# Latent attention with TensorE kept in program order, its last attention set apart, and modulation weights loaded two dot products ahead

## The chip, the cores and the metric

The kernel runs on one core of a Trainium2 chip. Its time is the device time of one execution in microseconds (us); three executions of the kernel before were timed, and one more was profiled. The core's engines are PE (TensorE, matrix products), DVE (VectorE), ACT (ScalarE), POOL (GpSimd) and SP (SyncE, which here only issues DMAs).

## The reference

One layer of a diffusion backbone for 256 latent tokens, with 256 context tokens ahead of them, of width 2048. What matters here:

```python
def reference(...):
    sh1, sc1, g1, sh2, sc2, g2 = jnp.split(jax.nn.silu(c) @ w_ada[l] + b_ada[l], 6, axis=-1)
    (lq_a, lkv_a, lk_r, ldq, ldk, ldv, ldz, lda, ldb, lga, lgb) = split_columns(
        modulate(rmsnorm(x, norm_mix[l]), sh1, sc1) @ w_in[l])
    ...
    k_l, v_l = mla_kv(lkv_a, lk_r, kv_a_norm[l], w_kv_b[l], k_norm[l], tabs)
    q_l = mla_q(lq_a, q_a_norm[l], w_q_b[l], q_norm[l], tabs)
    y_mla_l = attend_latent(q_l, k_l, v_l, k_c, v_c)
    ...
    o_dn_l, _ = dn_bidirectional(lq, lk, lv, lgd, lbeta, s_ctx, True)
    y_l = merge_branches(y_mla_l, dn_output(o_dn_l, ldz, ...), lga, lgb, w_o_mla[l], w_o_dn[l], w_out[l])
    x = x + jnp.expand_dims(g1, -2) * y_l
    x = x + jnp.expand_dims(g2, -2) * conv_glu(modulate(rmsnorm(x, norm_ffn[l]), sh2, sc2), ...)
```

`mla_kv` and `mla_q` normalise a latent of rank 512, multiply it up to 8 heads of 128 + 64 columns, normalise each head and rotate the last 64 columns (the rope). `attend_latent` is a softmax attention over 512 keys.

## The kernel before

**Stages.** By the trace the first projection and the first part of the modulation run to about 150 us, the heads of the gated DeltaNet to 440, the latent attention (MLA) from 440 to 743, the DeltaNet's scan to 957, the two branch projections and the output projection to 1145, and the feed-forward part to the end.

**Weights.** Every weight matrix comes as tiles of 128x1024 (`raw`, five places, shared with the `rawa` tiles below). `split` (L118) makes of each half of such a tile a rounded high part `whi` by a copy on ACT (L120) and the rest `wlo` by a subtraction on DVE (L121); there are six places for such halves. PE multiplies with both. All PE work goes through one helper, so that all its rows bear line 68.

**The latent attention.** Heads are taken in four pairs, b = 0 to 3. `mla_project(b)` (L984) makes keys (`k_head`, products `kps`), their norms (`ks`, `kbp`), values (`vps`), queries (`q_tile`, products `qps`) and the rotated parts of the queries (`rps`, which reads `qx`). `mla_attend(b)` (L1087) makes four tiles of scores (`sps`; two heads by two blocks of 128 queries). For each, DVE takes the maximum (L1102, L1104), ACT the exponential (L1105), DVE the reciprocal (L1106) and ACT the scaled row `s_` (L1107). `turn` transposes it on PE (`ptp`) and splits it into `PT` (ACT L120, DVE L121); `values` multiplies it with the values (`yps`) and sends the result to DRAM (`Ys`), from where it comes back as `yraw` and is split into `YM`.

**Side work.** Both generators give a number of ns at each `yield`, and `side(c, r)` (L1147) then issues as much of three other things: `fill`, the products `gtp` of z and gate tiles with the projected stream `h`, 24 tiles of 16 pairs of products; `inv`, products `ivp` of the blocks of an inverse that the scan needs (`off_diagonal`, L831, results to DRAM as `Xo`); and `ada`, the late modulation (`ada_rest`, L253). That is 128 dot products on DVE (L278) of a weight tile `rawa` with a row `sch`; each reads a tile that SP loads one dot ahead (L259). The loop at L1153 to L1162 first runs `mla_project(0)` through, then takes one step of `mla_project(b+1)` and one of `mla_attend(b)` by turns, seven times for each b. In the last round nothing is left to project.

**What sets the order.** A scheduler orders the instructions of every engine by its own times, where the code does not pin them. With `pe.pinned` True, PE's instructions stay in the order of the program; before the change that holds in the heads and in the scan, but not in the latent attention. Each engine then works through its order strictly, and an instruction that waits holds up those behind it. DVE, ACT and SP are left to the scheduler here.

Of the kernel before, what the change touches and what calls it, by code (L numbers as in the profile page):

```python
# [41 lines left out]
OC = 4000  # L42
# [11 lines left out]
def hybrid_block(ctx: ExitStack, tc: tile.TileContext, io, dbg=None):  # L54
# [20 lines left out]
    pe, oact, odve = (Ordered(e) for e in (nc.tensor, nc.scalar, nc.vector))  # L75
# [4 lines left out]
    def pool_(name, bufs, side="left"):  # L80
        return tc.tile_pool(name=name, bufs=bufs, side=side, reuse_waits="tile")
# [20 lines left out]
    half = const.tile([P, 1], F32, name="half")  # L102
# [150 lines left out]
    def ada_rest():  # L253


        def load(i):
            w = wr.tile([P, GR], F32, tag="raw", name="rawa", bufs=NR)
            c, n = divmod(i, 32)
            sync.dma_start(w, io["wada2"][c, (n // 16 + c) % 2, n % 16])  # L259
            return w  # L260

        parts = ad.tile([P, 2, 16], F32, name="parts")
        half, ahead = None, load(0)
        for i in range(128):
            c, n = divmod(i, 32)
            h, j = (n // 16 + c) % 2, n % 16
            if h != half:

                for _ in range(2 if i else 0):
                    yield 1300  # L270
                half, sch = h, ad.tile([P, GR], F32, tag="sch", name="sch")
                sync.dma_start(sch, Sc[h])
                for _ in range(4):
                    yield 1300
            w = ahead
            if i < 127:
                ahead = load(i + 1)
            dve.tensor_tensor_reduce(out=w, in0=w, in1=sch, scale=1.0, scalar=0.0, op0=ALU.mult, op1=ALU.add, accum_out=parts[:, h, j : j + 1])  # L278
            if n == 31:
                cs = slice(16 * c, 16 * c + 16)  # L280
                dve.tensor_tensor(out=adaT[:, cs], in0=parts[:, 0], in1=parts[:, 1], op=ALU.add)
                dve.tensor_tensor(out=adaT[:, cs], in0=adaT[:, cs], in1=bada[:, 32 + 16 * c : 48 + 16 * c], op=ALU.add)
                ada.done = c + 1
            yield 1300
# [124 lines left out]
    def load(*what):  # L409
        for kind, n in what:  # L410
            d, f = {"w": (wts, load_scale), "s": (shifts, load_shift), "g": (grs, load_first)}[kind]
            d[n] = f(n)
# [342 lines left out]
    def head_inputs(h, side=lambda c: None):  # L755
# [13 lines left out]
        return xs[0], xs[1], xq  # L769

    ada = Side(ada_rest())
    ada.done = 0
    ins = {h: head_inputs(h) for h in (3, 0)}
# [9 lines left out]
    for heads, nxt in (((3, 0), (4, 1)), ((4, 1), (5, 2)), ((5, 2), (6,)), ((6,), (7,)), ((7,), ())):  # L783
# [3 lines left out]
        def side(c):  # L787
            work(c * 17000 * len(heads) / main)
            ada(c * ADB / 22600)
# [41 lines left out]
    def off_diagonal():  # L831

        pI = ExitStack()
        pi = pI.enter_context(pool_("pj", 1, "right"))
        bd = [pi.tile([P, 4, P], F32, name=f"bd{n}") for n in range(2)]
        for n in range(2):
            pool.memset(bd[n], 0.0)

        def load(q):
            rs = slice(4 * q, 4 * q + 4)  # L840
            uo = pi.tile([P, 4, 32], F32, tag="uo", name="uo", bufs=2)
            sync.dma_start(uo, Uo[:, :, rs].rearrange("g j r i -> (g j) r i"))
            xd = pi.tile([P, 2, 4, 32], F32, tag="xd", name="xd", bufs=2)
            for n in range(2):
                sync.dma_start(xd[:, n], Xq[2 * n, rs].rearrange("r g j c -> (g j) r c"))
            return uo, xd

        ahead = load(0)
        yield OD
        for q in range(8):  # L850
            uo, xd = ahead
            if q < 7:
                ahead = load(q + 1)
            for n in range(2):
                src = uo if n == 0 else ip
                for g in range(4):
                    gs = slice(32 * g, 32 * g + 32)
                    act.copy(bd[n][gs, :, gs], src[gs])
                ip = psa.tile([P, 4, 32], F32, tag="aux", name="ivp")
                for r in range(4):  # L860
                    pe.matmul(ip[:, r], bd[n][:, r], xd[:, n, r], start=True, stop=True)
                if n == 0:
                    yield OC
            act.copy(uo, ip)
            act.dma_start(Xo[4 * q : 4 * q + 4].rearrange("r g c i -> (g c) r i"), uo)
            yield OC
        pI.close()

    Ys = dram.tile([P, HEADS, T], F32, name="Ys")
# [90 lines left out]
    pN.close()  # L960
    pc2 = pC.enter_context(pool_("pc2", 2))
    inv = Side(off_diagonal())

    def mm3(ps, a, b, first, last):
# [19 lines left out]
    def mla_project(b):  # L984
# [41 lines left out]
        def q_tile(j):  # L1026
            ps = psa.tile([P, 512], F32, tag="aux", name="qps")
            for k in range(4):
                mm_hl(ps, P, W(j * 512 + k * P), qan_[:, k], k == 0, k == 3)
            qx = pc2.tile([P, T], F32, tag="qx", name="qx")  # L1030
            gather(ps, P, qx)
            if j < 2:
                act.activation(qts[j][:, 0], qx, AF.Copy, scale=qkn)
                dve.scalar_tensor_tensor(out=qts[j][:, 1], in0=qx, scalar=qkn, in1=qts[j][:, 0], op0=ALU.mult, op1=ALU.subtract)
            act.activation(qsq[:, j], qx, AF.Square)
            return qx
# [25 lines left out]
            pass  # L1062
        yield 3500
        qx = q_tile(2)
        yield 1300
        rps = psa.tile([P, T], F32, tag="aux", name="rps")
        pe.matmul(rps, perm, qx, start=True, stop=True)
        rq = ryx[:, 0]
# [78 lines left out]
    def side(c, r):  # L1147
        fill(r * c)
        inv(r * c)
        ada(AD * c)  # L1150

    for c in mla_project(0):
        side(c, R0)  # L1153
    for b in range(4):
        at, pr = mla_attend(b), mla_project(b + 1) if b < 3 else iter(())
        for n in range(7):
            for st in (pr, at):
                c = next(st, None)
                if c is not None:
                    side(c, R1 if b < 3 else 2.0)  # L1160
        for _ in at:
            pass  # L1162
    inv.finish()
    fill.finish()
    gates = gate_tiles([("wgd", f, Gs[1, :, f], None) for f in range(KD)])
# [407 lines left out]
```

## Time and profile before

| | us |
|---|---|
| median of three executions | 1846.19 |
| lowest and highest | 1843.73, 1850.49 |
| the profiled execution | 1845.3 |
| its span in the trace | 1843.5 |
| PE busy | 1773.1 |
| DVE busy | 1366.4 |
| ACT busy | 917.9 |

All times of rows are of the profiled execution, in us from the start of its span, which lies 1.8 us within that execution's time. Rows of a timeline give start, duration, engine, line, operation, out<-in, partitions x elements, and in brackets the idle time just before the instruction and what ended it. Matrix products overlap: what one adds is the distance to the start of the next, not its duration.

### The profile page before, as it was taken

Reading aid. Unit: us, or ns where it says so; the run is one execution under the profiler, and the core shown is the slowest. Engines: PE = TensorE matmul, PEld = TensorE weight load, DVE = VectorE, ACT = ScalarE, POOL = GpSimd, SP = SyncE. Lnnn points to the kernel's source line nnn. Section 1 sums busy time; section 2 is a strip of 40 time slices with the busy share of each in tenths; the row PEclk is TensorE's granted clock in tenths of the full one; section 3 lists DMA queues with packets and bytes.
Section 4 is the critical chain, followed back from the end, with each engine's and each line's share of the span. In section 5 each row is a group of like instructions: output and inputs, shape, how many; then the busy total and the mean of one; then the engine's idle time right before and its main releaser. Section 6 shows DMA issues by size and latency. Waiting matters only on the chain.

```text
span 1843.5 us, 33058 instructions
## 1 busy us (share of the span) xinstructions
PE 1773.1 (96%) x12450; PEld 1525.7 (83%) x12450; DVE 1366.4 (74%) x2758; ACT 917.9 (50%) x1876; POOL 45.9 (2%) x48
## 2 busy tenths in 40 slices
PE   7999999999998999898999989999999999999999
PEld 5787887888887888777878877888888888888887
DVE  4668899879776877575779798888877788855554
ACT  3335544445666665433346445555555555544443
POOL 0000001000000000000000000000000000000000
PEclk9999999999999999999989999999999999999999
DMA  9883688774777767887766885777766677766664
GB/s 379 349 311 110 178 241 241 215 235 132 214 229 222 217 209 227 293 287 244 250 220 206 285 297 179 254 220 223 231 197 187 212 219 221 266 194 195 201 197 120
DMA packets 195009, 419.72 MB, mean 228 GB/s; under 512 B 61280, under 2 KB 101344, under 8 KB 192416
## 3 DMA queue, kind: packets, MB, share of 16 engines
q1 hardware_dynamic: 167520, 402.19, 68.0%
q10 hardware_dynamic: 27328, 15.41, 2.8%
q8 instruction: 98, 1.61, 0.4%
q14 instruction: 63, 0.52, 0.1%
HBM read 388.57 MB, written 28.84 MB: 226 GB/s over the span
## 4 chain that ended last, share of the span: by engine, by line
PE 48%; issue 9%; DVE 2%; DMA 2%; ACT 1%; POOL 0%; SPq 0%; POOLq 0%; ACTq 0%; DVEq 0%
PE fps L68 25%; PE dps L68 13%; PE gtp L68 4%; PE brp L68 2%; PE op L68 1%; DVE wlo L121 1%; DMA raw<-in_wgate 1%; PE yp L68 1%; DMA yraw<-Ys 0%; DVE r L1264 0%; PE kp L68 0%; ACT whi L120 0%; DMA Gs<-zx 0%; POOL om L172 0%; DMA raw<-in_wgd 0%
## 5 line engine op out<-in xcount | busy, mean ns | idle before, releaser
L121 DVE TENSOR_TENSOR wlo<-raw,whi 128x512 fp32r<-128x512 f32 (+1 forms) x940 | 634.5, 686 | 209.7 <-ACT whi L120 202.0
L120 ACT CAST whi<-raw 128x512 fp32r<-128x512 f32 (+1 forms) x940 | 572.9, 618 | 420.8 <-PE dps L68 112.4
L68 PE MATMUL fps<-H,whi 128*128 128x512 f32 x1376 | 481.5, 398 | 1.7 <-DVE H L1416 1.7
L68 PE MATMUL fps<-H,wlo 128*128 128x256 f32 x1376 | 374.3, 282 | 0.6 <-DVE wlo L121 0.6
L68 PEld LDWEIGHTS fps<-H,whi 128*128 128x128 f32 x1376 | 253.8, 189 | 57.9 <-issue 2.0
L68 PEld LDWEIGHTS fps<-H,wlo 128*128 128x128 f32 x1376 | 259.3, 188 | 8.7 <-DVE wlo L121 1.1
L68 PE MATMUL gtp<-h,whi 128*128 128x512 f32 x640 | 234.7, 402 | 5.1 <-ACT whi L120 5.1
L68 PE MATMUL mmp<-h,whi 128*128 128x512 f32 x640 | 228.9, 400 | 0.0
L68 PE MATMUL dps<-GB,whi 128*128 128x512 f32 x560 | 195.9, 391 | 0.0
L278 DVE CUSTOM_DVE_ANT_0 rawa<-rawa,sch 128x1024 f32<-128x1024 f32 x128 | 156.2, 1222 | 44.0 <-DMA rawa<-in_wada 43.1
L68 PE MATMUL gtp<-h,wlo 128*128 128x256 f32 x640 | 175.7, 285 | 5.5 <-DVE wlo L121 5.2
L68 PE MATMUL mmp<-h,wlo 128*128 128x256 f32 x640 | 176.6, 282 | 0.0
L68 PE MATMUL dps<-GB,wlo 128*128 128x256 f32 x560 | 155.3, 282 | 0.0
L68 PEld LDWEIGHTS gtp<-h,whi 128*128 128x128 f32 x640 | 120.8, 190 | 31.5 <-ACT whi L120 6.3
L68 PEld LDWEIGHTS mmp<-h,whi 128*128 128x128 f32 x640 | 119.1, 188 | 26.2 <-issue 0.4
L68 PEld LDWEIGHTS gtp<-h,wlo 128*128 128x128 f32 x640 | 121.3, 190 | 13.2 <-DVE wlo L121 8.7
L68 PEld LDWEIGHTS dps<-GB,whi 128*128 128x128 f32 x560 | 105.2, 188 | 21.7
L68 PEld LDWEIGHTS mmp<-h,wlo 128*128 128x128 f32 x640 | 120.5, 188 | 2.8 <-issue 0.6
L68 PEld LDWEIGHTS dps<-GB,wlo 128*128 128x128 f32 x560 | 105.9, 189 | 0.6
L68 PE MATMUL fp<-h,gh 128*128 128x256 f32 (+1 forms) x448 | 86.6, 291 | 7.9 <-DVE h L68 5.9
L68 PEld LDWEIGHTS fp<-h,gh 128*128 128x128 f32 (+1 forms) x448 | 69.2, 187 | 15.1 <-DVE h L68 8.0
L513 ACT COPY fx<-fps 128x256 f32<-128x256 f32 x86 | 31.9, 374 | 68.3 <-PE fps L68 68.2
(561 smaller groups left out, 2561.9 us busy)
## 6 DMA issues: line engine op xcount, KB each, us to landing
rawa<-in_wada SPq DMA_DIRECT2D x128, 512.0 KB, 4.7
raw<-in_wgate SPq DMA_DIRECT2D x82, 512.0 KB, 4.3
raw<-in_wval SPq DMA_DIRECT2D x82, 512.0 KB, 4.8
raw<-in_wdown SPq DMA_DIRECT2D x80, 512.0 KB, 4.3
wt<-in_wadas SPq DMA_DIRECT2D x16, 1024.0 KB, 9.9
raw<-in_wadab SPq DMA_DIRECT2D x32, 512.0 KB, 8.5
raw<-in_wgm SPq DMA_DIRECT2D x32, 512.0 KB, 4.9
raw<-in_wgd SPq DMA_DIRECT2D x32, 512.0 KB, 6.1
```

Of the source, the lines that this page charges most:

```text
L68: i = f(*a, **k)
L120: act.copy(hi, raw)
L121: dve.tensor_tensor(out=lo, in0=raw, in1=hi, op=ALU.subtract)
L278: dve.tensor_tensor_reduce(out=w, in0=w, in1=sch, scale=1.0, scalar=0.0, op0=ALU.mult, op1=ALU.add, accum_out=parts[:, h, j : j + 1])
L513: act.copy(out, ps[:M, T:])
```

## The change

Loads of `rawa` are issued two dots ahead of their use in place of one. `off_diagonal` gives half of its ns before each group of products instead of all after it (the sum stays). `mla_project` gives 2600 ns in place of 1300 between the last query tile and the rotation. PE is pinned from the latent attention on, and stays so through the scan. In the loop the attention of the pair before (`tail`) is given a step between the two others; after the loop there is a `side(2600, 1.0)`, and the rest of `tail` is run. Since `mla_attend` has seven yields and is given seven steps, what is handed over as `tail` has no work left.

```diff
-        half, ahead = None, load(0)
+        half, ahead = None, [load(0), load(1)]
...
-            w = ahead
-            if i < 127:
-                ahead = load(i + 1)
+            w = ahead.pop(0)
+            if i < 126:
+                ahead.append(load(i + 2))
...
+                yield OC / 2
                 ip = psa.tile([P, 4, 32], F32, tag="aux", name="ivp")
...
                 if n == 0:
-                    yield OC
+                    yield OC / 2
...
-            yield OC
+            yield OC / 2
...
         qx = q_tile(2)
-        yield 1300
+        yield 2600
         rps = psa.tile([P, T], F32, tag="aux", name="rps")
...
+    pe.pinned = True
     for c in mla_project(0):
         side(c, R0)
+    tail = iter(())
     for b in range(4):
         at, pr = mla_attend(b), mla_project(b + 1) if b < 3 else iter(())
         for n in range(7):
-            for st in (pr, at):
+            for st in (pr, tail, at):
                 c = next(st, None)
                 if c is not None:
                     side(c, R1 if b < 3 else 2.0)
-        for _ in at:
-            pass
+        tail = at
+    side(2600, 1.0)
+    for _ in tail:
+        pass
```

**The first keys, on PE.** Before, the twelve products of the first head's keys stand woven between products `gtp`:

```order
L68 MATMUL gtp<-h_308,whi 128x512
L68 MATMUL kps<-kvn,whi 128x512
L68 MATMUL gtp<-h_308,whi 128x512
L68 MATMUL gtp<-h_308,wlo 128x256
L68 MATMUL gtp<-h_308,whi 128x512
L68 MATMUL gtp<-h_308,wlo 128x256
L68 MATMUL gtp<-h_308,whi 128x512
L68 MATMUL kps<-kvn,whi 128x512
L68 MATMUL kps<-kvn,wlo 128x512
```

After, behind the same `gtp`, they are one block:

```order
L68 MATMUL gtp<-h_308,whi 128x512
L68 MATMUL kps<-kvn,whi 128x512 x2
L68 MATMUL kps<-kvn,wlo 128x512
L68 MATMUL kps<-kvn,whi 128x512 x2
L68 MATMUL kps<-kvn,wlo 128x512
L68 MATMUL kps<-kvn,whi 128x512 x2
L68 MATMUL kps<-kvn,wlo 128x512
L68 MATMUL kps<-kvn,whi 128x512 x2
L68 MATMUL kps<-kvn,wlo 128x512
```

The `gtp` that stood between have moved behind the block.

**The last attention (b = 3), on PE.** Before, the second transposition and what is around it (the `gtp` rows that are left out here are 15 more of the same two kinds in a row, behind the first score tile shown):

```order
L68 MATMUL ptp<-ident,s__8487 128x128 x4
L68 MATMUL sps<-kt,qt 128x512 x3
L68 MATMUL sps<-krt,qt 128x512 x2
L68 MATMUL gtp<-h_308,whi 128x512
...
L68 MATMUL ptp<-ident,s__8531 128x128 x4
L68 MATMUL sps<-kt,qt 128x512 x3
L68 MATMUL sps<-krt,qt 128x512 x2
L68 MATMUL ptp<-ident,s__8579 128x128 x4
L68 MATMUL gtp<-h_308,whi 128x512
L68 MATMUL gtp<-h_308,wlo 128x256
L68 MATMUL gtp<-h_308,whi 128x512
L68 MATMUL yps<-PT,V 128x512
```

After, from the second score tile on:

```order
L68 MATMUL sps<-kt,qt 128x512 x3
L68 MATMUL sps<-krt,qt 128x512 x2
L68 MATMUL ptp<-ident,s__8550 128x128 x4
L68 MATMUL sps<-kt,qt 128x512 x3
L68 MATMUL sps<-krt,qt 128x512 x2
L68 MATMUL ptp<-ident,s__8597 128x128 x4
L68 MATMUL sps<-kt,qt 128x512 x3
L68 MATMUL sps<-krt,qt 128x512 x2
L68 MATMUL ptp<-ident,s__8618 128x128 x4
L68 MATMUL yps<-PT,V 128x512
```

No `gtp` is left between them up to the last `yps`. Of the 58 that stood there before (16 + 16 + 3 + 14 + 9), 32 have moved ahead of this attention, into the longer steps before `rps`, and 26 behind it, where 96 follow in a row in place of 70. Before `rps` there stood 8 `gtp` behind the query tile in the rounds b = 0 and 1; now there are 16 and the 4 (`ivp`) of the inverse, and more.

**The dots in that attention, on DVE.** After, a dot stands between the maximum of a score and its reciprocal (L1107, L1106 before) twice; here is the second, for the score tile 8618:

```order
L121 TENSOR_TENSOR PT<-ptp,PT 128x4x128
L1103 ISA s__8618,mns<-kbc,sps 128x512
L1103 ISA mns 128x1
L1107 RECIPROCAL mns<-mns 128x1
L1105 TENSOR_SCALAR mns<-mns,qm 128x1
L278 ISA rawa,parts<-rawa,sch 128x1024
L278 ISA parts 128x1
L1107 RECIPROCAL mns<-mns 128x1
L121 TENSOR_TENSOR PT<-ptp,PT 128x4x128
```

Before, none stands between the two (those of this attention come behind a reciprocal). A third stands after between `qm` and `qt`, ahead of the first score tile.

**Loads and dots.** On SP the second load is issued right behind the first, and each later one an index earlier at its place. On DVE the dots have moved by one index too, so that the first now stands here, among the DeltaNet heads:

```order
 L666 SCALAR_TENSOR_TENSOR cy<-ct,cy 128x256
+L278 ISA rawa,parts<-rawa,sch 128x1024
+L278 ISA parts 128x1
 L121 TENSOR_TENSOR wlo<-raw,whi 128x512 x2
```

Between the load of a tile and the dot that reads it there stand in this stage and the next about as many weight halves as before (three, before four). When the attention's result `YM` is split, 58 dots stand ahead of it, before 54.

## Rows read from the trace of the kernel before

**Rows 1.** The page's busy times of the engines over the whole span, with their share of it and their instructions.

```profile
PE 1773.1 (96%) x12450; PEld 1525.7 (83%) x12450; DVE 1366.4 (74%) x2758; ACT 917.9 (50%) x1876; POOL 45.9 (2%) x48
```

**Rows 2.** The latent attention as one stretch: its length, busy time (and count) of PE, weight loads, DVE, ACT and POOL, granted clock, DMA share, GB/s.

```profile
440.00:743.00 303.00, 288.81 (x2211) 249.57 (x2209) 222.49 (x475) 193.81 (x435) 18.98 (x18) 0.99 0.71 216
```

**Rows 3.** Waits of PE in the same stretch: who waited for what, us in total, times, the longest.

```profile
PE yps L68 <- DVE PT L121: 3.4, 2, 2.7
PE rps L68 <- DVE qx L514: 2.9, 2, 2.0
PE yp L68 <- DMA jit<-Xo: 2.2, 1, 2.2
PE ks L68 <- ACT ksq L995: 2.1, 2, 1.9
```

**Rows 4.** Waits of DVE in the same stretch, the largest.

```profile
DVE rawa L278 <- DMA rawa<-in_wada: 27.5, 22, 5.1
```

**Rows 5.** PE's timeline around the second of the two waits for `qx`, in round b = 1; the first row is the first of eight products `gtp` behind the query tile.

```profile
631.99 0.40 PE L68 MATMUL gtp<-h,whi 128*128 128x512 f32 x1
...
633.41 0.60 PE L68 MATMUL ptp<-ident,s__7451 128*128 128x128 f32 x4
635.97 0.70 PE L68 MATMUL rps<-qx,rope 128*128 128x256 f32 x2 [1.97 <-DVE qx L514]
...
637.11 0.64 PE L68 MATMUL gtp<-h,whi 128*128 128x512 f32 x1
...
641.33 0.39 PE L68 MATMUL gtp<-h,whi 128*128 128x512 f32 x1
```

**Rows 6.** DVE's timeline, ahead of PE's longest wait for `PT` (first row) and just ahead of that `rps`.

```profile
570.71 1.23 DVE L278 CUSTOM_DVE_ANT_0 rawa<-rawa,sch 128x1024 f32<-128x1024 f32 x1 [5.13 <-DMA rawa<-in_wada]
...
634.35 1.22 DVE L278 CUSTOM_DVE_ANT_0 rawa<-rawa,sch 128x1024 f32<-128x1024 f32 x1
...
635.50 0.42 DVE L514 TENSOR_TENSOR qx<-qps,qx 128x256 f32<-128x256 f32 x1
```

**Rows 7.** Three stretches at the lower granted clock, columns as in rows 2: the two of the latent attention, and one at the end of the output projection.

```profile
572.46:575.87 3.41, 3.27 (x10) 2.79 (x11) 2.45 (x8) 2.03 (x6) 1.18 (x1) 0.50 0.62 234
637.32:640.73 3.41, 3.41 (x11) 2.85 (x11) 2.12 (x7) 1.00 (x3) 1.11 (x1) 0.50 1.02 393
...
1104.94:1115.18 10.24, 5.57 (x32) 4.65 (x33) 7.20 (x18) 3.74 (x9) 0.70 (x1) 0.50 0.33 102
```

**Rows 8.** PE's timeline at the first keys: the first product of the first head, and three of the second head's.

```profile
455.55 0.50 PE L68 MATMUL kps<-kvn,whi 128*128 128x512 f32 x1
...
463.36 0.63 PE L68 MATMUL kps<-kvn,whi 128*128 128x512 f32 x2
...
464.06 0.63 PE L68 MATMUL kps<-kvn,whi 128*128 128x512 f32 x2
```

**Rows 9.** DVE's timeline there: the last of the four rows of the latent, normalised, and its low part.

```profile
458.44 0.74 DVE L955 SCALAR_TENSOR_TENSOR kvx<-kvx,vecs,bk 128x512 f32<-128x512 f32 x1
...
460.30 0.69 DVE L121 TENSOR_TENSOR kvn<-kvx,kvn 128x512 fp32r<-128x512 f32 x1
```

**Rows 10.** ACT's timeline: the high part of that row, and the squares of the first head's keys with the instruction ahead of them that waited.

```profile
459.51 0.62 ACT L120 CAST kvn<-kvx 128x512 fp32r<-128x512 f32 x1 [0.41 <-DVE kvx L955]
...
472.71 0.37 ACT L513 COPY zx<-gtp 128x256 f32<-128x256 f32 x1 [3.15 <-PE gtp L68]
...
473.90 0.58 ACT L995 ACTIVATE ksq<-kps 128x512 f32<-128x512 f32 x1
```

**Rows 11.** PE's timeline in the last attention: the first transposition, the third score tile, the product behind it, and the first product with the values.

```profile
710.34 0.60 PE L68 MATMUL ptp<-ident,s__8487 128*128 128x128 f32 x4
710.69 0.94 PE L68 MATMUL sps<-kt,qt 128*128 128x512 f32 x3
...
711.93 0.39 PE L68 MATMUL gtp<-h,whi 128*128 128x512 f32 x1
...
718.36 1.69 PE L68 MATMUL yps<-PT,V 128*128 128x512 f32 x8 [0.68 <-DVE PT L121]
```

**Rows 12.** DVE's timeline there: the maximum of that third score tile, and the low part of its `PT`.

```profile
713.55 0.68 DVE L1102 CUSTOM_DVE_ANT_0 s__8579<-kbc,sps 128x512 f32<-128x512 f32 x1
...
718.83 0.69 DVE L121 TENSOR_TENSOR PT<-ptp,PT 128x512 fp32r<-128x512 f32 x1
```

**Rows 13.** ACT's timeline there: the scaled row of the tile, and the high part of its `PT`.

```profile
715.66 0.73 ACT L1107 ACTIVATE s__8579<-s__8579,mns 128x512 f32<-128x512 f32 x1
...
718.07 0.57 ACT L120 CAST PT<-ptp 128x512 fp32r<-128x512 f32 x1
```

**Rows 14.** The chain of waits behind the last attention, in order of time: start, us, what.

```profile
726.90 4.00 DMA Ys<-ryx
730.92 7.82 DMA yraw<-Ys
738.76 1.91 ACT YM L120
740.69 2.30 DVE YM L121
```

**Rows 15.** PE's timeline at the end of the latent attention: the first products of the scan's side, and the first of the branch projection.

```profile
740.51 2.02 PE L68 MATMUL yp<-jit 128*128 128x128 f32 x16 [2.15 <-DMA jit<-Xo]
743.04 0.50 PE L68 MATMUL brp<-YM,whi 128*128 128x512 f32 x1 [0.51 <-DVE YM L121]
```

## Prediction

> **What bounds the kernel now.** I read the busy times first: PE works for 1773.1 of 1843.5 us [rows 1], so the kernel is PE's order of work and the gaps in it. A gain can only come from gaps of the stretch that is changed. The stretch of the latent attention is 303.0 us long with PE busy for 288.8 [rows 2], so at most 14.2 us are to be had there, 0.8% of the whole. The list of PE's waits says what the gaps are: `PT` 3.4 us, `qx` 2.9, the inverse coming back from DRAM 2.2, `ksq` 2.1 [rows 3]. The engine behind most of them is DVE, and DVE's own list says why: it waits 27.5 us in 22 places for a `rawa` tile that has not landed [rows 4]. Since DVE keeps to its order, a dot that waits for its tile holds up the subtraction that PE needs: the dot at 570.71 waited 5.13 us, and PE's longest wait, 2.7 us for `PT`, ended just behind it [rows 3, 6].
>
> Two more things are to be seen in the stretch. The granted clock fell to 0.50, its lower level of 1.2 GHz, for 3.41 us twice, each time behind one of the two longest waits, that of 2.73 us and that of 1.97 us [rows 3, 5, 7]; behind the 2.15 us wait for the inverse no such stretch follows. And the work that fills PE's gaps, `gtp`, is a fixed amount: what is moved into one gap is missing in another.
>
> **The change part by part.** The sum is made against the profiled execution (1845.3 us), which lies 0.9 below the median of 1846.2, so that a change of zero reads 1845.3 to 1846.2.
>
> *The longer step before `rps`.* In rounds 0 and 1 `rps` waited for `qx`, 2.9 us in two places [rows 3]. In the second, 8 `gtp` from 631.99 to 633.41 and one transposition lay between the query tile and `rps` at 635.97, and the rest was the wait [rows 5]; on DVE a dot of 1.22 us stood right ahead of `qx` [rows 6]. Eight `gtp` take 1.42 us, 0.178 each. The new order puts 16 of them there, the inverse's products and a transposition, over 3.2 us in place of 1.4 and what the latter two take, so the first wait (0.9) goes surely and the second, with 1.97, as good as: **-2.9**. The lower clock behind the second goes with it. 3.41 us at half the clock hold at most 1.7 us of lost work, and the products there were pushed to 0.64 from 0.39 us [rows 5, 7]: **-1.5** (0 to -1.7).
>
> *The pinned first keys.* Before, twelve products for the first head were woven between `gtp` from 455.55 on [rows 8]; three of them take 0.70 us, so all take 2.8. In a block they would end at 458.35. But the last row of the latent is only normalised at 458.44, has its high part at 459.51 and its low part at 460.30 to 460.99 [rows 9, 10], and DVE's and ACT's orders there have hardly moved. The low part is read by the last three products, so the block ends at about 461.5: **+3.1** in waits. The bounds are 0, if that row comes sooner once the `gtp` gathers around it are later, and +4.6, if the wait also brings a stretch of lower clock like the two above.
>
> *The squares of the first head.* `ks` waited up to 1.9 us [rows 3], since on ACT a gather of a `gtp` tile that was not done stood ahead of `ksq` (3.15 us of waiting) [rows 10]. One such gather less stands there now: **-1.1** (0 to -1.9).
>
> *The last attention.* This is the dear part. From the maximum of a score to its finished row take 713.55 to 716.39, 2.84 us [rows 12, 13]; the high and low parts of `PT` add 0.57 and 0.69. A transposition costs PE 0.35 us and a score tile 1.24 [rows 11]. Before, 16 `gtp` (2.8 us) stood behind each of the first three scores, and they and the next score hid the chain; the wait that was left was 0.68 at the first `yps` [rows 11]. Now only the first tile has them. The second row must be ready 0.35 + 1.24 = 1.6 us after its score, against 2.84 and some time for the engines to take turns: 1.3 to 1.8 us of waiting. The third has the same two pieces and the wait before it: about 0.6. The products with the values then wait for `PT`, 0.57 + 0.69 less what lies between, 1.2 and 1.3, and the first transposition may wait 0.8 for its exponential, behind a weight half that finds no free place. Together 5.7, against 0.7 in the same places before: **+5.0** (bounds +1.2, if only the wait for the second row is left, and +8, if none of the waits overlaps with another).
>
> *Behind it.* The chain by `Ys` and `yraw` to `YM` takes from 726.90 to 742.99, 16.1 us, and the gather ahead of it [rows 14]. Before, 70 `gtp` covered it and PE waited 2.15 and 0.51 us in the end [rows 15]. Now 96 do; the 26 more are 26 x 0.178 = 4.6 us, and both waits go: **-2.7**. So of the 26 products that left the attention over half comes back here.
>
> *The loads two ahead.* The text asks for a dot's tile one index sooner. But DVE's order follows what the scheduler takes as landed: dot and load both moved one index, and between them stand about as many halves as before. So the 27.5 us of waits on `rawa`, 1.25 each in 22 places, stay, and with them the long wait for `PT`, its lower clock, and the smaller waits: 0, between -4.9 (the waits for `PT` and the lower clock behind the longest gone) and +5 (another one like the longest). Three dots now stand at worse places, in the last attention: one ahead of `qt` and so of the first score, 1.23 us of its own: **+1.2**; two between a maximum and its reciprocal, where nothing hides them any more; if one of them waits the mean of 1.25, and partly beside PE's work: **+1.0** (0 to +10). Four dots fewer are left for the scan and the output projection, whose other work keeps its order: 0, with ±4 for what their places there do.
>
> *`tail`, the split `yield` of the inverse:* 0. The first has no work; the second keeps its sum, and the inverse's transfers have 16 us more of cover at the end, as above.
>
> Sum: -2.9 - 1.5 + 3.1 - 1.1 + 5.0 - 2.7 + 1.2 + 1.0 = **+2.1**. That is 1847.4 against the profiled execution and 1848.3 against the median; I say **1847**. A difference of 0.5% (9 us) is about what a measurement of this kernel can tell from no change; this is well inside.
>
> **The rivals.**
>
> *The loads do come a dot sooner (faster).* If the tiles have landed when DVE gets to the dots, the waits for `PT` (3.4) and its lower clock (1.5) go beside those for `qx`, and the dots of the last attention cost only their 1.23: 1847.4 - 3.4 - 1.5 - 1.0 = 1841.5; if the first keys hide their wait as well, 1838.4, and with the 4 us that the later dots may give, 1834. That needs DVE's waits on `rawa` to fall from 27.5 to a few us. For it: the code asks for it, and most of PE's waits have this source. Against it: the new order moved each dot with its load. And even this ends at the edge of what can be told.
>
> *The last attention stalls on dots (slower).* The two dots between maximum and reciprocal have no cover. If each waits like the longest, 5.13 us [rows 6], PE stands for 10.2 us more, in pieces of over 2 us between short groups of products. The granted clock has been at 0.50 behind such waits, and for 10.24 us at a stretch where PE was busy for only 5.57 of them [rows 7]; at half the clock such a stretch costs up to 5.1. Then 1847.4 - 1.0 + 10.2 + 5.1 = 1861.7; with one dot late and 3.41 us of lower clock, 1847.4 - 1.0 + 5.1 + 1.7 = 1853.2. It decides the sign from two dots that wait over 4 us each. Against it: of 22 waits the mean is 1.25 us. The Trainium skill ("TensorE: Matmul & The Clock Gate", section "HAM oscillation — how this bites in real kernels") speaks for it: idle gaps between short groups of matmuls send the clock to half its rate again and again, so that each group starts cold. The trace agrees in two places of the stretch and disagrees in one (2.15 us, no drop); by that rule every gap of the last attention would count, which is this rival.
>
> *The change does little of what it says.* `tail` is empty, and the loads' lead does not grow. This is not beside the forecast; it is part of it.
>
> **How the numbers follow.** The forecast, waits shifted and about even: 0.72, 1839 to 1855. The faster rival 0.14, of which some 0.10 lies below 1837, with what the scan's dots may add; the slower one 0.14, all but a little above 1855. The range of 8 in 10 takes in the unknown terms: 1847.4 less 3.1 (keys hidden), 3.8 (the attention's lower bound) and 2 (half of what the later dots may give) is some 1838, and 1847.4 plus 3 (its upper bound), 1.5 (clock at the keys) and 5 (one late dot) some 1857: 1838 to 1857. Faster by over 0.5% (below 1837) 0.10, within it 0.76, slower (above 1855.4) 0.14.
>
> **What would show it.** In the profile after: no wait of `rps` for `qx`; a block of twelve `kps` near 456 to 462 with waits for `kvn`; in the last attention waits of `ptp` for `s_` and of `yps` for `PT` of 4 to 7 us together, and none of `yp` for `jit` or `brp` for `YM` behind it; DVE's waits on `rawa` in this stretch still over 20 us. It would be wrong if those fall under 10 us (then faster), if the clock is at 0.50 for over 10 us in the last attention (then slower), or if a stage after 743 us changes by more than 4 us.

## The result and the profile after

The changed kernel takes 1855.8 us (median of six; 1850.1 to 1864.2), the kernel before 1846.9 beside it: a ratio of 1.0048, 95% interval 1.0030 to 1.0066. Measured once more on another occasion it was 1.0044 (1.0025 to 1.0063). It is slower by some 8 to 9 us, within the stated range of 1838 to 1857 and just inside the half per cent, but well above the forecast of 1847. The profiled execution, 1850.1 us with a span of 1848.3, is the shortest of the six, so its trace shows about half of the loss (its span is 4.8 us longer than before); the second profile (1858.0 us) is used beside it. One execution of that second occasion, 2474.7 us at a mean granted clock of 0.652, is left out of its ratio.

Waits of PE in the latent attention, after (columns as in rows 3):

```profile
PE ptp L68 <- ACT s__8618 L1108: 3.3, 1, 3.3
PE ptp L68 <- ACT s__8550 L1108: 2.0, 1, 2.0
PE ks L68 <- DVE mns L1103: 1.9, 1, 1.9
PE ptp L68 <- ACT s__8597 L1108: 1.7, 1, 1.7
PE yps L68 <- DVE PT L121: 1.4, 1, 1.4
PE ks L68 <- ACT ksq L996: 1.3, 3, 0.8
PE ptp L68 <- ACT s__8641 L1108: 1.1, 1, 1.1
PE kps L68 <- ACT kvn L120: 1.1, 1, 1.1
PE kps L68 <- DVE kvn L121: 1.1, 2, 0.7
```

All waits of [rows 3] for `qx`, for `jit` and the long one for `PT` are gone. In their place stand the four rows `s_` of the last attention and one `PT`, 9.5 us together, and a wait of `ks` in the third pair, 1.9 us in place of 1.2 before. PE's timeline there shows them one after another, and the products slower towards the end:

```profile
706.90 0.63 PE L68 MATMUL sps<-krt,qt 128*128 128x512 f32 x2
709.48 0.66 PE L68 MATMUL ptp<-ident,s__8550 128*128 128x128 f32 x4 [1.95 <-ACT s__8550 L1108]
...
712.97 0.66 PE L68 MATMUL ptp<-ident,s__8597 128*128 128x128 f32 x4 [1.67 <-ACT s__8597 L1108]
...
718.07 0.66 PE L68 MATMUL ptp<-ident,s__8618 128*128 128x128 f32 x4 [3.28 <-ACT s__8618 L1108]
718.48 2.09 PE L68 MATMUL yps<-PT,V 128*128 128x512 f32 x8
721.65 1.12 PE L68 MATMUL ptp<-ident,s__8641 128*128 128x128 f32 x4 [1.08 <-ACT s__8641 L1108]
724.17 2.93 PE L68 MATMUL yps<-PT,V 128*128 128x512 f32 x8 [1.40 <-DVE PT L121]
```

The last `yps` takes 2.93 us against 1.69 of the first one before [rows 11]: the granted clock is at 0.50 there, for as long as the third stretch of [rows 7] (columns as there):

```profile
719.47:729.71 10.24, 7.75 (x25) 6.04 (x24) 2.31 (x5) 2.86 (x7) 2.42 (x3) 0.50 0.22 74
```

The longest wait has a dot behind it. DVE's timeline, between the maximum of the third score and its reciprocal:

```profile
712.12 0.21 DVE L1105 TENSOR_SCALAR mns<-mns,qm 128x1 f32<-128x1 f32 x1
715.95 1.23 DVE L278 CUSTOM_DVE_ANT_0 rawa<-rawa,sch 128x1024 f32<-128x1024 f32 x1 [3.62 <-DMA rawa<-in_wada]
717.10 0.08 DVE L278 DVE_READ_ACCUMULATOR2_ANT parts<- 128x1 f32 x1
717.10 0.16 DVE L1107 RECIPROCAL mns<-mns 128x1 f32<-128x1 f32 x1
```

Over the stretch, DVE still waits over 20 us for tiles of the dots (27.5 us in [rows 4]), and for their row `sch` in one place:

```profile
DVE rawa L278 <- DMA rawa<-in_wada: 21.8, 16, 3.6
...
DVE rawa L278 <- DMA sch<-Sc: 2.2, 1, 2.2
```

Behind the attention the two waits of [rows 15] are gone:

```profile
745.08 1.95 PE L68 MATMUL yp<-jit 128*128 128x128 f32 x16
746.78 0.48 PE L68 MATMUL brp<-YM,whi 128*128 128x512 f32 x1
```

The first branch product starts at 746.8, before at 743.0. From there to the first product of the feed-forward part it is 367.6 us (1114.4), before 368.2 (1111.2), and from there to the end 733.9, before 732.3.

In what follows the attention is measured from the first `kps` to the first `brp`: 287.5 us before (455.5 to 743.0), 290.6 in the first profile after (456.2 to 746.8), 295.6 in the second (461.0 to 756.6). So of the 4.8 us that the first profile is longer, 3.1 lie in the attention, 0.7 ahead of it and 1.6 in the feed-forward part, less 0.6 between. Of the 12.7 us of the second, 8.1 lie in the attention and 5.5 ahead of it. What makes it start later is not shown: the eight profiles with the loads two ahead have their first `kps` between 455.4 and 461.0 us, the six without between 455.2 and 457.9.

### The profile page after: what moved, and what is told of

The parts are those of the page before. It is cut to its first block, busy times and chain, and to the rows that moved or that the text cites. A ratio compares the mean times of both kernels' runs of the same rounds, so it can differ in the third digit from the quotient of the medians.

```text
span 1848.3 us, 33065 instructions
## 1 busy us (share of the span) xinstructions
PE 1776.0 (96%) x12450; PEld 1527.2 (83%) x12450; DVE 1365.3 (74%) x2758; ACT 919.4 (50%) x1876; POOL 45.4 (2%) x48
## 4 chain that ended last, share of the span: by engine, by line
PE 76%; issue 10%; DVE 6%; DMA 5%; ACT 2%; POOL 1%; SPq 0%; ACTq 0%; POOLq 0%; DVEq 0%
PE fps L68 26%; PE dps L68 13%; PE mmp L68 11%; PE gtp L68 9%; PE brp L68 2%; PE fp L68 2%; DMA rawa<-in_wada 2%; DVE wlo L121 1%; PE op L68 1%; PE amp L68 1%; PE vps L68 1%; PE qps L68 1%; PE tp L68 1%; DVE rawa L278 1%; DMA raw<-in_wgd 1%
```

## The experiments

The theory: the loss is the last attention, whose chain of score, row and `PT` lies bare on PE, with the dots in it and the clock that falls behind it. The rivals: the dots alone; the pinning as such; the longer steps as such; or the loads.

**The changed kernel again**, without an edit.

> The changed kernel as it is, once more, beside the next three: its time and a second trace. Theory (bare last attention): again 8 to 11 us of waits of ptp and yps there and a stretch of at least 6.8 us at the lower clock behind or among them; 1852 to 1858. Rival (the first trace was a chance of late loads): waits under 6 us there, no long stretch of lower clock, and a time that differs from the first by more than 5 us.

Ratio 1.0044. Waits of PE in the last attention, and the clock behind them:

```profile
PE ptp L68 <- ACT s__8618 L1108: 2.8, 1, 2.8
PE ptp L68 <- ACT s__8550 L1108: 1.7, 1, 1.7
PE ptp L68 <- ACT s__8597 L1108: 1.7, 1, 1.7
PE yps L68 <- DVE PT L121: 1.4, 1, 1.4
PE ptp L68 <- ACT s__8641 L1108: 1.1, 1, 1.1
```

```profile
728.45:738.69 10.24, 7.75 (x26) 5.97 (x25) 2.41 (x6) 3.35 (x7) 0.98 (x2) 0.50 0.17 58
```

8.7 us in the same five places and again 10.24 us at the lower clock, so neither is a chance of one execution.

**The last attention left to the scheduler.**

```diff
     for b in range(4):
+        pe.pinned = b < 3
         at, pr = mla_attend(b), mla_project(b + 1) if b < 3 else iter(())
```

> The changed kernel with TensorE's order pinned only through the first three pairs; in the last attention the scheduler may weave the gate products between the scores again. Theory (the bare chain of the last attention is the loss: 9.5 us of waits and a stretch of 10.24 us at half the clock in the changed kernel's profile): the waits for s_ fall under 2 us, the clock stays up there, and the time falls to 1842 to 1848, about that of the kernel before. Rival (the loss lies elsewhere in the stretch or in what follows it): the waits fall in the same way, but the time stays over 1852.

1848.9 us, ratio 1.0011 (0.9996 to 1.0026). The waits for `s_` fell to 1.3 and 0.8, and 1.6 and 1.0 us for `jit` and `YM` are back behind it:

```profile
PE yp L68 <- DMA jit<-Xo: 1.6, 1, 1.6
PE ptp L68 <- ACT s__8550 L1108: 1.3, 1, 1.3
PE brp L68 <- DVE YM L121: 1.0, 1, 1.0
PE ptp L68 <- ACT s__8618 L1108: 0.8, 1, 0.8
```

No lower clock lies in the last attention:

```profile
707.94:730.69 22.75, 20.63 (x114) 16.72 (x112) 18.14 (x43) 16.20 (x33) 0.00 (x0) 1.00 0.70 220
```

By the ratios most of the loss is gone with the pinning of this one part, though the two intervals just meet.

**The side products of the first three pairs given out more slowly**, so that some are left for the last:

```diff
-R1 = 1.0
+R1 = 0.85
```

> The changed kernel with the side products of the first three pairs given out at 0.85 of the pace, so that the last attention has 16, 16, 24 and 24 of them behind its scores and 16 behind the first values, and the scan loses none. Theory (missing cover is the loss, and the earlier pairs have some to spare): waits of ptp and yps in the last attention under 3 us, no long lower clock there, the scan as before: 1845 to 1849. Rival (the earlier pairs need what they have): the last attention is mended, and 4 us or more of waits open in the first three pairs, so that the time stays over 1851.

1847.5 us, ratio 1.0002 (0.9983 to 1.0021), with pinning, loads and steps as in the changed kernel. PE's waits from 695 us to the first branch product, in full:

```profile
PE yps L68 <- DVE PT L121: 1.9, 1, 1.9
```

and the stretch with its granted clock:

```profile
700.00:742.70 42.70, 40.83 (x240) 35.53 (x238) 28.12 (x54) 25.74 (x52) 2.74 (x3) 1.00 0.80 252
```

The attention takes 284.5 us. With the cover back, the loss is gone, and one number does it. The edit is not of the cover alone: `side` gives out the inverse's products by the same number. It does not beat the kernel before: other waits opened in an earlier pair (below, the dot near 520 us).

**Two of the later gate tiles given to the last attention.**

```diff
-    fill = Side(gate_tiles([...] + [("wgm", f, Gs[0, :, f], None) for f in range(KD)]))
+    fill = Side(gate_tiles([...] + [("wgm", ...) for f in range(KD)] + [("wgd", f, Gs[1, :, f], None) for f in range(2)]))
...
-    gates = gate_tiles([("wgd", f, Gs[1, :, f], None) for f in range(KD)])
+    gates = gate_tiles([("wgd", f, Gs[1, :, f], None) for f in range(2, KD)])
```

> The changed kernel with two of the later gate tiles given to the side work of the latent attention, so that 16, 16, 24 and 24 products stand behind the four scores of the last attention in program order, and 96 behind it as before. Everything else of the change stays. Theory (the missing cover is the loss): the waits for s_ are gone but for the last (under 3 us with yps), no long stretch of lower clock there, and 6 to 9 us of the loss come back: 1846 to 1850. Rival (pinning, first keys or the dots elsewhere are the loss): the time stays over 1852; a second rival, that the two tiles are missed in the scan: the waits go, and 4 us or more come back in the scan's stretch.

1853.6 us, ratio 1.0030 (1.0014 to 1.0047). The waits there fell to one group, 2.6 us, with the clock at 1.00:

```profile
PE yps L68 <- DVE PT L121: 2.6, 2, 1.6
```

```profile
700.00:753.70 53.70, 51.06 (x339) 43.95 (x338) 37.24 (x76) 31.18 (x63) 3.85 (x4) 1.00 0.76 244
```

But in the first 217 us from the first branch product on, the changed kernel has the clock at 0.98 and 1559 products,

```profile
746.80:963.80 217.00, 200.89 (x1559) 173.48 (x1558) 148.59 (x360) 80.53 (x167) 4.56 (x4) 0.98 0.79 267
```

and this one 0.94 and 1494:

```profile
753.70:970.70 217.00, 196.96 (x1494) 169.60 (x1492) 142.96 (x349) 74.25 (x154) 4.51 (x4) 0.94 0.77 263
```

Of the 65 fewer, 64 are the products of the two tiles, 11.4 us of work at 0.178 each. Even so the scan, from the first `brp` to the first product of the second branch, takes 219.0 us (753.7 to 972.7), in the changed kernel 216.3 (746.8 to 963.1). The cover was taken from the scan and missed there: the second rival, and the gain was given back later. This profile (1858.9 us) is the longest of its twelve executions.

**No dots in the last attention.**

```diff
-    def side(c, r):
+    def side(c, r, d=AD):
...
-        ada(AD * c)
+        ada(d * c)
...
-                    side(c, R1 if b < 3 else 2.0)
+                    side(c, R1 if b < 3 else 2.0, 0 if (b, n) >= (2, 5) else AD)
...
-    side(2600, 1.0)
+    side(2600, 1.0, 0)
```

> The changed kernel without modulation dots in the last attention (they are put off into the scan and after); TensorE's order there stays bare. Theory (the bare chain decides, the dots add to it): of the 9.5 us of waits the 3.6 us behind the late dot and some of 1.2 go, 5 to 6.5 us stay, and the clock still falls; the time is 1849 to 1853. Rival (the dots decide): waits under 3 us, no lower clock, 1843 to 1848.

1850.0 us, ratio 1.0022 (1.0007 to 1.0036). PE's waits in the last attention:

```profile
PE ptp L68 <- ACT s__8591 L1108: 2.0, 1, 2.0
PE yps L68 <- DVE PT L121: 1.4, 1, 1.4
PE ptp L68 <- ACT s__8632 L1108: 1.1, 1, 1.1
```

4.5 us, and the clock still fell, for 6.83 us from 719.29. By the two ratios the bare chain alone is about half of the loss and the dots in it the other half; the intervals leave room for a sixth as well as for four fifths.

**Pinning alone.**

```diff
+    pe.pinned = True
     for c in mla_project(0):
         side(c, R0)
```

> The kernel before with nothing but the pinning of TensorE from the latent attention on. Its last attention keeps 16 products behind each of the first three scores, and loses the 26 around the values. Theory: waits of 2 to 4 us at the last transposition and values, no long stretch of lower clock there, the wait for the inverse gone: within 4 us of the kernel before. Rival (the pinning as such is the loss, wherever the cover lies): 6 us or more above it.

1849.1 us, ratio 1.0002 (0.9992 to 1.0013). Here the last attention keeps its products behind the first three scores; `yps` waits 2.8 us and one `ptp` 1.5, the wait for the inverse is gone, and the granted clock stays at 1.00 from 700 to 743 us. Pinning as such costs nothing that can be told.

**Loads two ahead alone.**

```diff
-        half, ahead = None, load(0)
+        half, ahead = None, [load(0), load(1)]
...
+            w = ahead.pop(0)
+            if i < 126:
+                ahead.append(load(i + 2))
```

> The kernel before with nothing but the loads two dots ahead. Theory (dot and load move together, the lead stays): VectorE's waits on rawa in the latent attention stay between 20 and 30 us and the time within 3 us of the kernel before. Rival (the loads do come sooner): these waits fall under 10 us and the time by 4 us or more.

Ratio 1.0011 (0.9999 to 1.0022). DVE's waits:

```profile
DVE rawa L278 <- DMA rawa<-in_wada: 25.5, 19, 5.8
```

Against 27.5 in 22 places [rows 4]: the lead did not grow, and the time cannot be told from that of the kernel before.

**The longer step alone.**

```diff
         qx = q_tile(2)
-        yield 1300
+        yield 2600
```

> The kernel before with nothing but the longer step before rps (TensorE is not pinned, so the scheduler may weave what is left into the last attention). Theory: the waits for qx (2.9 us) go; but 32 products fewer are left for the last attention and come back as waits there and in the steps behind; 0 to 4 us above the kernel before. Rival (the scheduler makes good for it): 2 to 5 us under it.

Ratio 1.0022 (1.0004 to 1.0040), 4 us slower. One wait for `qx` of 0.4 us is left of 2.9, and others stand in its place: `yp` for the DeltaNet's keys 3.6, `ks` for `km` 3.4, a `ptp` of the last attention 2.0. The attention takes 290.9 us in place of 287.5. What it gives to `rps` is lost elsewhere; that the products moved are what each of these waits misses is argued, not shown.

**The longer step and the divided yield, without pinning and without the loads.**

```diff
-    pe.pinned = True
     for c in mla_project(0):
         side(c, R0)
...
-        half, ahead = None, [load(0), load(1)]
+        half, ahead = None, load(0)
```

> The changed kernel without the pinning and with the loads one dot ahead: what stays is the longer step before rps and the divided yield of the inverse. Theory: the waits for qx are gone (2.9 us before) without the wait at the first keys; what the last attention loses of its cover to the longer steps (26 of 58 products) is woven again: 1843 to 1847. Rival (the cover that is used up earlier is the loss, pinned or not): 1851 or more.

Ratio 1.0020 (1.0006 to 1.0033). The theory had expected a gain; 1851.9 us is the rival's figure. Waits of 3.0 us of `ks` for `km` and of `yp` for the DeltaNet's keys stand there as in the run above. But the attention takes 287.3 us, as long as before (287.5), so the profile does not show the rival's mechanism: its 6.6 us lie ahead of the attention (2.2), from there to the feed-forward part (2.5) and in that part (2.1).

**The short step, all else of the change kept.**

```diff
-        yield 2600
+        yield 1300
         rps = psa.tile([P, T], F32, tag="aux", name="rps")
```

> The changed kernel with the step before rps back at 1300 ns, and nothing else undone: 16 products stand again behind each of the first three scores of the last attention, none behind the fourth. Theory (the longer steps use up the products that the last attention is short of): its waits fall from about 9 to 5 us, no stretch of 10.24 us at the lower clock, rps waits for qx again by 2 to 3 us; 1848 to 1851, 3 to 7 us under the changed kernel. Rival (the pinning or the loads make the loss): over 1853.

Ratio 1.0043 (1.0024 to 1.0063): no gain, against the theory. The waits of the last attention did fall, to 4.4 us, since 16 products stand behind three scores again; `rps` waits for `qx` again, 1.4 us. But the clock was at 0.50 there all the same, and for as long again at 528:

```profile
528.20:538.50 10.30, 8.04 (x62) 7.44 (x63) 7.54 (x22) 4.99 (x12) 2.01 (x2) 0.50 0.70 206
726.20:736.40 10.20, 7.72 (x26) 5.94 (x25) 3.93 (x9) 2.85 (x6) 2.00 (x3) 0.50 0.55 182
```

Ahead of the first lies a dot of the first pair:

```profile
521.06 1.23 DVE L278 CUSTOM_DVE_ANT_0 rawa<-rawa,sch 128x1024 f32<-128x1024 f32 x1 [4.09 <-DMA rawa<-in_wada]
```

PE's products `vps` waited 2.5 us behind it. A dot at 521 to 527 us waited 3.6 to 4.3 us in five of the nine profiles with the divided yield (this one, the second of the changed kernel, the last attention left to the scheduler, and both with the spread side products), with a stretch of lower clock behind each; in the other four and in all kernels without the divided yield none there waited over 2.5. What sets it off was not isolated. Nor is it enough for the loss: both kernels with the spread side products have it and are level with the kernel before.

PE's order in the last attention is here the same as with pinning alone, whose ratio is 1.0002. What the two kernels differ in is the loads, the divided yield and the `side(2600, 1.0)` behind the loop, and what the profiles differ in is the clock more than the waits: over the whole execution it is at 0.50 for some 58 us here, 41 with pinning alone, 34 in the kernel before and 41 and 44 in the two profiles of the changed kernel. The median of the executions' mean clock is 0.986 here, beside 0.989 of the kernel before; in the changed kernel's second measurement both are 0.988.

**Fewer dots in the attention, more in the scan, in the kernel before.**

```diff
-AD = 0.55
+AD = 0.3
...
-ADS = 0.3
+ADS = 0.5
```

> The kernel before with the modulation dots taken at 0.3 in place of 0.55 of the pace in the latent attention, and at 0.5 in place of 0.3 in the scan, so that 40 in place of 54 are done when the scan begins. Theory (waits of the attention come from dots that wait for their tile): VectorE's waits on rawa there fall from 27 to about 15 us and PE's waits for PT and qx by half, 2 to 5 us less in this stretch, and up to as much lost in the scan: 1843 to 1848. Rival (late tiles are no cause): waits of PE in the attention unchanged.

Ratio 1.0004 (0.9991 to 1.0016). The attention took 280.8 us, 6.7 less than before; from the first `brp` to the feed-forward part it took 374.6, 6.4 more. DVE's waits fell only to 21.2 us where 15 were expected. The dots do cost the attention that much, and the scan and what follows it charge the same.

**Spread side products, one load ahead, no dots in the last attention.**

```diff
-R1 = 1.0
+R1 = 0.85
...
-        half, ahead = None, [load(0), load(1)]
+        half, ahead = None, load(0)
...
-                    side(c, R1 if b < 3 else 2.0)
+                    side(c, R1 if b < 3 else 2.0, 0 if (b, n) >= (2, 5) else AD)
```

> The same with the loads one dot ahead and no modulation dots in the last attention: the best that the runs so far point to. Theory (cover and dots are the two halves of the loss): no waits over 1.5 us in the last attention, 1843 to 1847, at or under the kernel before. Rival (what the dots cost is paid in the scan): 1848 or more, with waits of over 2 us more in the scan than before.

1846.6 us, ratio 1.0004 (0.9987 to 1.0022). In its last attention only `yps` waits, 1.9 us. It is level with the kernel before; no run of this study beats that.

**All runs beside one another.** The attention is taken as above. The last attention is the time from its first score to the end of its last `yps`, less 0.178 us for each `gtp` between: an estimate of what is left of it without the filling work. The last column is the time at 0.50 that begins in it. Each row but for its ratio is one execution.

| kernel | ratio | attention, us | last attention, us | at 0.50, us |
|---|---|---|---|---|
| before | 1 | 287.5 | 10.8 | 0 |
| changed | 1.0048 | 290.6 | 22.1 | 10.2 |
| changed, again | 1.0044 | 295.6 | 22.1 | 10.2 |
| last attention left to the scheduler | 1.0011 | 289.3 | 12.2 | 0 |
| side products at 0.85 | 1.0002 | 284.5 | 11.2 | 0 |
| two later gate tiles (64 products more) | 1.0030 | 292.8 | 10.9 | 0 |
| no dots in the last attention | 1.0022 | 286.5 | 15.9 | 6.8 |
| pinning alone | 1.0002 | 287.3 | 14.9 | 0 |
| loads alone | 1.0011 | 292.6 | 10.7 | 0 |
| longer step alone | 1.0022 | 290.9 | 13.8 | 3.4 |
| longer step and divided yield | 1.0020 | 287.3 | 12.0 | 0 |
| short step | 1.0043 | 296.8 | 17.4 | 10.2 |
| fewer dots, kernel before | 1.0004 | 280.8 | 11.0 | 0 |
| side products at 0.85, one load, no dots | 1.0004 | 284.0 | 11.9 | 3.4 |

## Why the prediction held, and where it was mis-sized

The range held the time and the sign of the sum was right; its size, +2.1 us, was a quarter of what was measured. That the range held is owed to its upper end, which took in the attention's upper bound and one late dot; both came, and with them the prediction's own sign of a slower kernel, over 10 us at 0.50 in the last attention. The waits there, 9.5 and 8.7 us, were also above the 4 to 7 that it gave.

- *The longer step* did what was forecast: no wait for `qx`, and no lower clock behind the second. Against that, 3.4 us at the lower clock stand in a new place, from 600 us, behind the wait of `ks` of 1.9 us. That the step helps (-2.9 and -1.5) was only half of it. Alone it made the kernel 4 us slower; the side products are a fixed amount, as the prediction said, which then priced what is missed in the last attention only.
- *The first keys:* 2.2 us of waits for `kvn` against +3.1, as the order had shown.
- *The squares:* the first head's wait for `ksq` fell from 1.9 to 0.8 us in both profiles, -1.1 as forecast. In the second profile another wait for `ksq`, 2.2 us in the second pair, takes it back.
- *The last attention* is the step that failed in size: +5.0 for the chain and +1.0 for late dots, against 9.5 us of waits less 0.7, plus the clock. The second transposition was put at 1.3 to 1.8 us and measured 1.7. The first was put at 0.8 and measured 2.0 and 1.7. The third was put at 0.6 and measured 3.3 and 2.8, since its dot waited 3.62 us for its tile, and 3.13 in the second profile. The products with the values were put at 1.2 and 1.3; the first did not wait, the last did for 1.4, and the 1.1 us of the fourth transposition stood in no term. The clock was left to the slower rival. Not every gap counted for it: behind the first two waits, 1.95 and 1.67 us, it stayed up, and it fell at 719.47, behind the third. At 0.50 the last `yps` alone lost 1.2 us and the gate products behind it, at a pitch of 0.64 for a pair against 0.35, some 1.3 of the 2.8 us from 726.89 to 729.71.
- *The dot ahead of `qt`:* +1.2 was its time on DVE, and PE did not wait for it. The rope part of the first score (`sps<-krt,qt`) waited 0.27 us for `qt` before, and no such wait is listed after.
- *The slower rival* named this mechanism and so came half true: one dot late by over 3 us, not two by 5, and the lower clock of 10.24 us. Its one-dot figure, 1853, is between the two profiled executions (1850 and 1858).
- *Behind it:* both waits gone, -2.7 as forecast.
- *Loads two ahead:* the waits on `rawa` fell from 27.5 to 21.8 and 23.0 us, not under 10; alone the loads change nothing that can be told. The long wait for `PT`, which the sum let stand, was not there; 2.7 us more on the good side, so the rest of the loss was larger than the sum by that much as well. By the table above the last attention lost 11.3 us with its waits and its slower products, where the sum had 7.2 for it with its dots.
- *The faster rival* did not come: dot and load moved together.

Shown by two edits of different kinds is the cause in the last attention: weaving it again (1.0011) and saving products for it (1.0002) each take its 22.1 us to 12.2 or less, and the time from 1.0044 or more to about that of before. Not settled is the part outside it: the run with the short step mends half of the last attention's waits and is not faster, and pinning alone, with the same order of products there, is level. A dot of the first pair, late by about 4 us in five of nine profiles with the divided yield, costs PE 2 to 4 us and a stretch of lower clock. The divided yield by itself was not run, so it stands as an untested rival for that part.

## What to carry to other kernels

Filling work is a budget: before a step is lengthened, look at which later chain loses its cover, and price that chain with every engine that stands in it, not only its own operations. A load that is written earlier is no lead if the scheduler moves its reader by the same amount; read the distance between the two in the order before counting on it. And spreading the cover more evenly (one number) repaired what the longer step and the pinning together had exposed, while borrowing it from the next stage only moved the loss.

## What was not expected of the hardware

Much the same waits, between the same products in the same order, were followed by the lower clock in one kernel and not in another. At the end of the last attention with the short step (0.50 from 726.20 to 736.40, shown above):

```profile
725.41 2.27 PE L68 MATMUL yps<-PT,V 128*128 128x512 f32 x8 [1.95 <-DVE PT L121]
728.76 1.12 PE L68 MATMUL ptp<-ident,s__8635 128*128 128x128 f32 x4 [1.08 <-ACT s__8635 L1108]
731.28 2.93 PE L68 MATMUL yps<-PT,V 128*128 128x512 f32 x8 [1.40 <-DVE PT L121]
```

With pinning alone, where the granted clock stays at 1.00:

```profile
717.57 1.68 PE L68 MATMUL yps<-PT,V 128*128 128x512 f32 x8 [1.45 <-DVE PT L121]
720.79 0.66 PE L68 MATMUL ptp<-ident,s__8633 128*128 128x128 f32 x4 [1.54 <-ACT s__8633 L1107]
722.85 1.68 PE L68 MATMUL yps<-PT,V 128*128 128x512 f32 x8 [1.40 <-DVE PT L121]
...
700.00:743.00 43.00, 38.36 (x219) 32.31 (x218) 26.25 (x53) 24.35 (x47) 3.44 (x4) 1.00 0.69 203
```

Single executions of the changed kernel lie between 1849 and 1864 us, those of the kernel before between 1839 and 1854. Within a kernel the longer ones tend to have the lower mean clock: with the side products at 0.85 the shortest took 1835.8 us at 0.995 and the longest 1853.2 at 0.987. So where the clock falls may be part of this spread; no trace of those executions shows it.
